# Two gate projections moved into the spectral part of a mixer, three filter spectra kept in DRAM, spectral sums in buffers of their own, Fourier and inverse tiles in alternation

## The chip, the core and the metric

The kernel runs on one core of a Trainium2 chip. Its engines work side by side, each on its own queue of instructions in a fixed order: TensorE (PE) multiplies matrices into PSUM, VectorE (DVE) and GpSimd (POOL) do elementwise work (POOL only on SBUF), ScalarE (ACT) does activations and copies, and SyncE (SP) issues the DMAs. The metric is the time of one execution on the device in microseconds, the median of several runs.

## The reference, cut to what matters

The program is a two-layer block on a sequence `x` of 512 tokens and a context of 256 tokens, 1024 features. Layer 0 mixes with a Fourier half and a hyena half, layer 1 with attention; each layer ends with a convolutional feed-forward. Only the mixer of layer 0 is changed; it is applied to `x` and to the context with the same weights:

```python
def _long_conv(u, spectrum, bias):
    L = u.shape[1]
    u32 = _f32(u)
    y = jnp.fft.irfft(jnp.fft.rfft(u32, n=2 * L, axis=1) * spectrum[None], n=2 * L, axis=1)[:, :L]
    return (y + u32 * _f32(bias)).astype(u.dtype)

def _fourier_hyena_mixer(h, w_in, w_out, conv_w, conv_b, w1, b1, w2, b2, w3, b3, w4, freq, hy_bias):
    B, L, _ = h.shape
    proj = h @ w_in
    u_f = _f32(proj[..., :D_FOURIER]).reshape(B, L, N_FOURIER_GROUPS, FOURIER_GROUP_DIM)
    y_f = jnp.fft.fft2(u_f, axes=(1, 3), norm='ortho').real.reshape(B, L, D_FOURIER).astype(h.dtype)
    u_h = _dwconv3(proj[..., D_FOURIER:], conv_w, conv_b)
    x0, x1, v = jnp.split(u_h, 3, axis=-1)
    spectrum = _hyena_filter_spectrum(L, w1, b1, w2, b2, w3, b3, w4, freq)
    y_h = x0 * _long_conv(v * x1, spectrum, hy_bias)
    return jnp.concatenate([y_f, y_h], axis=-1) @ w_out
```

`_hyena_filter_spectrum` runs a small network over the positions, weighs its two-sided output with a decay, normalizes it and takes its Fourier transform. All of this is computed with matrices of cosines and sines. `x0`, the first third of the hyena projection, is the gate: it is needed only at the very end, where it multiplies the result of the long convolution.

## The kernel before, in words

Features lie on the 128 partitions and tokens on the free axis; a tile of width `TW` = 772 holds the 512 tokens of `x`, two zeros, the 256 of the context and two zeros. Every product in full precision is three matmuls (`mm3`, L123 to L125): each operand is split into a high part (ACT, `hi`, L98) and a low part (`lo`, L103, on DVE unless POOL is named). `wload` loads a weight tile of 512 KB into one of three raw buffers (`wr`) and splits it into one of three pairs `wh` and `wl`. PSUM has three tiles `mm` of two banks and two tiles `ms` of one.

The mixer (L459) runs in this order.

- Norms, modulation and the first three input projections, in an order written out by hand (`manual_schedule`). After it the order on each engine is made by a planner, which takes work by the order of the program text where it is ready and has buffers by its own estimate of times; so later work can run ahead as filler.
- The filter: `time_tile` (L575) makes six tiles over time (4 and 5 for the context, 0 to 3 for `x`), each with a decay tile from DRAM (`dec`). Each output tile of the input projection is 48 matmuls over eight feature tiles and two column parts (`proj`, L563); `hconv` (L571) adds the three-tap convolution (`conv3`: one ACT and two DVE instructions, L322 to L324) and some modulation sums (`gemv_dve`: a 512 KB load, then per condition a DVE sum L210 and an addition L211). `filter_spec` (L432) transforms the filter, one frequency tile (`ft`) at a time, and `filter_scale` (L443) scales it into a pair `hr`, `hi`: two pairs for the context (`Hc`), four for `x` (`H`). Gate tiles 4 and 5 are projected between the time tiles, 6 and 7 after the first and second spectrum of `x` (L607).
- Eight more projections in pairs 12 + i and 8 + i (L637 to L644). `fold` multiplies the pair (POOL) and folds it (DVE, L623 and L624), and `turn` transposes it (L630) into `uTh` and `uTl`. Then `tm`, the pool of these tiles, and `hp`, the projections' input `hh` and `hl`, are closed, and the outputs `yh` and `yl` (pool `yp`) take the place of `hp`; `zero_pads` writes their pads with 32 POOL memsets.
- `spectral` (L656) transforms the folded input by one frequency tile and multiplies it by the filter: per tile two parts `c`, each with two DVE products from PSUM (L676, L677 or L680, L681, and a single row L683 for the Nyquist term `ny`), a POOL sum (L678 or L684), a high part on ACT and a low part, on DVE for `c` = 0 and on POOL for `c` = 1. It is run for the context (two tiles, `Yc`), then `inverse` (L693) and `hy_out` (L706: `e` and `s`, the gate and the split into `yh`, `yl`) four times for the context, then `spectral` for the four tiles of `x`.
- `fourier(g)` (L739) for three groups, the four inverse tiles of `x` with `hy_out`, and the fourth group. A group splits its input into `fuh` and `ful`, transforms over features into PSUM, splits that into `pqh` and `pql` (six parts: four of `x`, two of the context), transforms over time and writes its output rows. `fuh`, `ful`, `pqh` and `pql` have one buffer each.
- `res_proj` then projects with `w_out` over the eight tiles of `yh` and `yl`.

All of this shares one pool of small tiles, `S2`, with 19 buffers of 128x512 (tag `s2`): decay tiles, time tiles, `hr` and `hi`, `ny`, the `a` and `b` of the spectral products, their high and low parts (`Yc`, 8 buffers; `Y`, 16), `e` and `s`, and `e` and `y` of the Fourier groups.

Of the kernel before, what the change touches and what calls it, by code (L numbers as in the profile page):

```python
# [9 lines left out]
F32 = mybir.dt.float32  # L10
# [8 lines left out]
P = 128  # L19
D = 1024  # L20
KD = 8
# [29 lines left out]
class Builder:  # L51
# [407 lines left out]
    def mixer(self):  # L459
# [124 lines left out]
        with self.tc.issue_after(last.ins), self.tc.issue_after(last_act.ins):  # L584
# [24 lines left out]
        self.dbg("H", H, Hc, ny, nyc)  # L609
# [27 lines left out]
        for i in range(4):  # L637
# [6 lines left out]
            folded.append(fold(i, cv, cx))  # L644
        turn(3, folded.pop())
        self.dbg("u", uTh, uTl, Uf, x0)
        self.close("tm")
        self.close("hp")


        yp = self.pool("yp", side="right")
        yh = [self.t(yp, [P, TW], F32R, f"yh{m}") for m in range(KD)]
        yl = [self.t(yp, [P, TW], F32R, f"yl{m}") for m in range(KD)]
        self.zero_pads(yh + yl)

        def spectral(fts, Hs, ny, kp, km, nt):  # L656

            Y = []
            for ft, (hr, hi) in zip(fts, Hs):
# [46 lines left out]
        def hy_out(i, ps, n, c0):  # L706

            e = self.t(self.S2, [P, 512], F32, "s2")
            nc.scalar.copy(e[:, :n], ps[:, :n])
            s = self.t(self.S2, [P, 512], F32, "s2")  # L710
# [7 lines left out]
        Yc = spectral((0, 1), Hc, nyc, 4, 5, 1)  # L718
# [5 lines left out]
        Y = spectral((0, 1, 2, 3), H, ny, 0, 2, 2)  # L724
# [14 lines left out]
        def fourier(g):  # L739
# [4 lines left out]
            pqh = self.t(pF, [P, 6, 256], F32R, "pqh", 1)  # L744
            pql = self.t(pF, [P, 6, 256], F32R, "pql", 1)
            for tt0, nt, sc in ((0, 4, None), (4, 2, math.sqrt(2.0))):
                ps = self.mm()
                for a in range(nt):
                    c = 128 * (tt0 + a) + (2 if tt0 else 0)
                    self.mm3(ps[:, 256 * a : 256 * a + 256], uh[:, c : c + 128], ul[:, c : c + 128], csh, csl, True, True)  # L750
                dh = pqh[:, tt0 : tt0 + nt, :].rearrange("p a b -> p (a b)")
# [688 lines left out]
```

## Time and profile before

| | us |
|---|---|
| median of 3 runs | 1829.6 (1828.78 to 1830.51) |
| the profiled execution | 1830.64 |
| its span, first to last instruction | 1828.8 |
| PE busy in the span | 1706.3 |
| DVE busy in the span | 1022.0 |
| ACT busy in the span | 613.9 |
| POOL busy in the span | 121.3 |

The span is cut into 40 slices of 45.7 us; a digit is the busy share of a slice in tenths, 9 for 90% or more, and PEclk is the granted PE clock in the same way. A table of stretches gives each engine's busy time between two times, with the number of instructions in brackets, then the clock, the share of the DMA engines and GB/s. A row of waits names who waited, `<-` for whom, and the total in us, the number of waits and the longest. A row of the timeline is the start in us, the duration in us, engine, line, instruction, output `<-` inputs by tile name, shapes, and in brackets the idle time before it and what ended it. Times are from the span's start.

### The profile page before, as it was taken

The page shows a single profiled execution, that of the slowest core. Times are in us where ns is not written, and L with a number is a line of the kernel's source. Part 1 is how long each engine was busy: PE and PEld are TensorE (multiplying, and loading weights), DVE is VectorE, ACT ScalarE, POOL GpSimd, SP SyncE. Part 2 cuts the span into 40 slices and gives each one's busy share as a digit, 9 for nine tenths or more (in the row PEclk, how much of TensorE's full clock was granted, in tenths as well). Part 3 has the DMA queues.
Part 4 walks back from the last instruction along what each step waited for, and adds up shares of the span by engine and source line. Part 5 has one row for each costly group of instructions (what it writes and reads, how often), then busy time and mean ns, then how long its engine had stood idle before and what let it go on. Part 6 is the DMA issues. An engine that isn't in the chain of part 4 may idle for free.

```text
span 1828.8 us, 21719 instructions
## 1 busy us (share of the span) xinstructions
PE 1706.3 (93%) x8742; PEld 1326.3 (73%) x8742; DVE 1022.0 (56%) x1662; ACT 613.9 (34%) x830; POOL 121.3 (7%) x202
## 2 busy tenths in 40 slices
PE   6889975799899999999999887899998999999999
PEld 2657864787688888888888556555554777888887
DVE  3486966864898435543434554665764554444443
ACT  3332222323323212222122434655663443223231
POOL 0052113310000000000000000110110000000000
PEclk7799987899999999999999998899999999999999
DMA  9032520352355234431312310000002323322322
GB/s 351 24 127 71 171 78 30 103 173 81 116 174 176 88 104 140 147 128 70 121 47 85 117 60 24 1 12 12 12 12 70 116 72 101 104 93 92 104 75 98
DMA packets 53249, 172.83 MB, mean 95 GB/s; under 512 B 6043, under 2 KB 8925, under 8 KB 52125
## 3 DMA queue, kind: packets, MB, share of 16 engines
q1 hardware_dynamic: 53149, 171.45, 27.4%
q8 instruction: 69, 1.13, 0.2%
q14 instruction: 31, 0.25, 0.0%
HBM read 167.23 MB, written 4.19 MB: 94 GB/s over the span
## 4 chain that ended last, share of the span: by engine, by line
PE 77%; DVE 11%; ACT 5%; POOL 3%; issue 3%; DMA 1%; POOLq 0%; SPq 0%; ACTq 0%; DVEq 0%
PE mm L123 21%; PE mm L124 20%; PE mm L125 20%; PE pv L1176 2%; PE ms L234 2%; PE z L1164 2%; DVE junk L210 2%; DVE wl L103 1%; DVE S L1154 1%; PE s L1130 1%; ACT S L1145 1%; PE s L123 1%; PE s L124 1%; PE s L125 1%; POOL s L388 1%
## 5 line engine op out<-in xcount | busy, mean ns | idle before, releaser
L123 PE MATMUL mm<-hh,wh 128*128 128x512 f32 (+2 forms) x1344 | 474.7, 356 | 7.0 <-ACT wh L98 3.4
L124 PE MATMUL mm<-hl,wh 128*128 128x512 f32 (+2 forms) x1344 | 473.9, 353 | 4.9 <-DVE hl L271 4.6
L125 PE MATMUL mm<-hh,wl 128*128 128x512 f32 (+2 forms) x1344 | 473.2, 353 | 1.3 <-DVE wl L103 1.3
L98 ACT ACTIVATE wh<-wr 128x1024 fp32r<-128x1024 f32 (+2 forms) x200 | 206.2, 1031 | 717.5 <-PE mm L124 646.5
L103 DVE TENSOR_TENSOR wl<-wr,wh 128x1024 fp32r<-128x1024 f32 (+2 forms) x200 | 243.6, 1219 | 287.3 <-ACT wh L98 279.6
L123 PEld LDWEIGHTS mm<-hh,wh 128*128 128x128 f32 x1344 | 254.4, 190 | 57.1 <-issue 12.0
L124 PEld LDWEIGHTS mm<-hl,wh 128*128 128x128 f32 x1344 | 255.0, 190 | 42.9 <-DVE hl L271 7.5
L125 PEld LDWEIGHTS mm<-hh,wl 128*128 128x128 f32 x1344 | 254.5, 190 | 38.4 <-issue 2.5
L123 PE MATMUL mm<-ah,wh 128*128 128x512 f32 (+1 forms) x528 | 187.8, 356 | 0.0
L124 PE MATMUL mm<-al,wh 128*128 128x512 f32 (+1 forms) x528 | 187.7, 356 | 0.0
L125 PE MATMUL mm<-ah,wl 128*128 128x512 f32 (+1 forms) x528 | 187.3, 355 | 0.0
L210 DVE SCALAR_TENSOR_TENSOR junk<-wr,sb 128x1024 bf16<-128x1024 f32 x128 | 159.3, 1244 | 36.7 <-DMA wr<-wmodT 36.6
L808 DVE SCALAR_TENSOR_TENSOR xr<-mm,mod,xr 128x512 f32<-128x512 f32 (+1 forms) x100 | 62.2, 642 | 204.3 <-PE mm L125 204.0
L123 PEld LDWEIGHTS mm<-ah,wh 128*128 128x128 f32 x528 | 99.1, 188 | 19.2 <-DVE xr L808 2.5
L124 PEld LDWEIGHTS mm<-al,wh 128*128 128x128 f32 x528 | 99.2, 188 | 15.3 <-issue 0.8
L125 PEld LDWEIGHTS mm<-ah,wl 128*128 128x128 f32 x528 | 99.2, 188 | 14.6
L1145 ACT ACTIVATE S<-s,rks 128x512 f32<-128x512 f32 x96 | 63.4, 688 | 44.3 <-PE s L125 43.4
L1154 DVE TENSOR_TENSOR S<-S,mb 128x1536 f32<-128x1536 f32 x32 | 54.8, 1752 | 20.7 <-POOL mb L1151 20.7
L845 ACT ACTIVATE fg<-fg 128x772 f32<-128x772 f32 (+1 forms) x44 | 32.6, 741 | 100.3 <-DVE fg L324 89.3
L1176 PE MATMUL pv<-S,V 128*64 128x512 f32 x192 | 58.9, 620 | 0.0
L1164 PE MATMUL z<-S,ones 128*32 128x512 f32 x192 | 42.7, 699 | 13.7 <-ACT S L1155 11.3
L1155 ACT ACTIVATE S<-S 128x1536 f32<-128x1536 f32 x32 | 47.1, 1481 | 18.0 <-DVE S L1154 18.0
(318 smaller groups left out, 2282.6 us busy)
## 6 DMA issues: line engine op xcount, KB each, us to landing
wr<-w_up SPq DMA_DIRECT2D x88, 512.0 KB, 3.3
wr<-wmodT SPq DMA_DIRECT2D x80, 512.0 KB, 3.3
wr<-w_dn SPq DMA_DIRECT2D x32, 512.0 KB, 3.2
wm<-wmod0a SPq DMA_DIRECT2D x8, 1024.0 KB, 9.6
wr<-w_in SPq DMA_DIRECT2D x16, 512.0 KB, 3.2
wr<-w_dn SPq DMA_DIRECT2D x20, 384.0 KB, 3.1
wr<-w_out SPq DMA_DIRECT2D x12, 512.0 KB, 3.2
wr<-w_o SPq DMA_DIRECT2D x12, 512.0 KB, 3.2
```

Of the source, the lines that this page charges most:

```text
L98: self.nc.scalar.activation(dst, src, AF.Copy)
L103: (eng or self.nc.vector).tensor_tensor(dst, src, hi.bitcast(F32), op=ALU.subtract)
L123: mmul(out, wh, xh, start=start, stop=False)
L124: mmul(out, wh, xl, start=False, stop=False)
L125: mmul(out, wl, xh, start=False, stop=stop)
L210: nc.vector.scalar_tensor_tensor(junk, raw, 1.0, self.sb[:, j, :], op0=ALU.mult, op1=ALU.mult, accum_out=acc)
L808: nc.vector.scalar_tensor_tensor(x[m][:, a2:b2], ps[:, a2:b2], mod[:, 8 * sec + m, j : j + 1], x[m][:, a2:b2], op0=ALU.mult, op1=ALU.add)
L1145: nc.scalar.activation(S[j // 3][:, j % 3, :], ps, AF.Copy, scale=rs[:, 2 * j + a : 2 * j + a + 1])
L1154: v.tensor_tensor(s, s, mb3.to_broadcast([P, 3, T]), op=ALU.subtract)
L1155: nc.scalar.activation(s, s, AF.Exp)
L1164: nc.tensor.matmul(z[32 * g : 32 * g + 32, :], self.ones32, Ss[g // 2][(2 * k + g % 2) // 3][:, (2 * k + g % 2) % 3, :], start=k == 0, sto ...
L1176: nc.tensor.matmul(pv[64 * a : 64 * a + 64, :], V[:, k, 64 * h : 64 * h + 64], Ss[a][k // 3][:, k % 3, :], start=k == 0, stop=k == 5, tile ...
```

## The change

- The four decay tiles of `x` are loaded after the context's time tiles, not each at its own use.
- The scaled filter spectra of `x` for the frequency tiles 1, 2 and 3 are stored to a DRAM pool `dr` (`Hd`, six tiles) and loaded again after the context's `spectral`. All pairs stand in one dictionary `Hs` (0 and 1 for the context, 2 to 5 for `x`), and `spectral` takes a pair out as it uses it.
- Gate projections 6 and 7 leave the filter stage. 6 stands ahead of the last `turn`, 7 behind the context's `spectral`; `hp` is closed, and `yp` opened, only after 7.
- The `a` and `b` of the spectral products and the context's `e` and `s` come from a new pool `Sx` with seven buffers.
- `pqh` and `pql` become two tiles each, one for the four parts of `x` and one for the two of the context.
- The Fourier groups 1, 2 and 3 each follow an inverse tile of `x`, in place of groups 0, 1, 2, then all inverse tiles, then group 3.
- The attention's DRAM pool is renamed.

The matmuls and their operands are the same.

```diff
         def time_tile(tt):
-            if tt not in dec:
-                dec[tt] = tp()
-                nc.sync.dma_start(dec[tt], I["decay"][tt])
             pm, f = self.filter_pm(self.filter_mm(h3, tt), dec[tt], tt in (0, 4))
...
             self.load_sb()
+            for tt in range(4):
+                dec[tt] = tp()
+                nc.sync.dma_start(dec[tt], I["decay"][tt])
...
-        Hc = [self.filter_scale(self.filter_spec(ac, tb), Sc) for tb in tbc]
+
+        dr = self.pool("dr", space=bass.MemoryType.DRAM)
+        Hd = {i: [self.t(dr, [P, 512], F32, f"Hd{i}{c}") for c in range(2)] for i in range(3, 6)}
+        Hs = {i: self.filter_scale(self.filter_spec(ac, tb), Sc) for i, tb in enumerate(tbc)}
...
-        H = []
         for ft in range(4):
-            H.append(self.filter_scale(self.filter_spec(ax, self.wload(I["ftab"][ft])), S))
+            parts = self.filter_scale(self.filter_spec(ax, self.wload(I["ftab"][ft])), S)
             if ft == 0:
+                Hs[2] = parts
                 ny = self.filter_nyquist(ax, S)
-            if ft < 2:
-                hconv(6 + ft, x0[2 + ft], 1)
+            else:
+                for c in range(2):
+                    nc.sync.dma_start(Hd[2 + ft][c], parts[c])
...
             folded.append(fold(i, cv, cx))
+        hconv(6, x0[2], 1)
         turn(3, folded.pop())
         self.close("tm")
-        self.close("hp")
-
-        yp = self.pool("yp", side="right")
-        yh = [self.t(yp, [P, TW], F32R, f"yh{m}") for m in range(KD)]
-        yl = [self.t(yp, [P, TW], F32R, f"yl{m}") for m in range(KD)]
-        self.zero_pads(yh + yl)
-
-        def spectral(fts, Hs, ny, kp, km, nt):
+        Sx = self.pool("Sx", bufs=7)
+        tx = lambda: self.t(Sx, [P, 512], F32, "sx")
+
+        def spectral(fts, h0, ny, kp, km, nt):
             Y = []
-            for ft, (hr, hi) in zip(fts, Hs):
+            for ft in fts:
+                hr, hi = Hs.pop(h0 + ft)
...
                 for c in range(2):
-                    a = self.t(self.S2, [P, 512], F32, "s2")
-                    b = self.t(self.S2, [P, 512], F32, "s2")
+                    a, b = tx(), tx()
...
         def hy_out(i, ps, n, c0):
-            e = self.t(self.S2, [P, 512], F32, "s2")
+            e, s = (tx(), tx()) if n == 128 else (tp(), tp())
             nc.scalar.copy(e[:, :n], ps[:, :n])
-            s = self.t(self.S2, [P, 512], F32, "s2")
...
-        Yc = spectral((0, 1), Hc, nyc, 4, 5, 1)
+        Yc = spectral((0, 1), 0, nyc, 4, 5, 1)
+        hconv(7, x0[3], 1)
+        for i in range(3, 6):
+            Hs[i] = [tp() for _ in range(2)]
+            for c in range(2):
+                nc.sync.dma_start(Hs[i][c], Hd[i][c])
+        self.close("hp")
+        yp = self.pool("yp", side="right")
+        yh = [self.t(yp, [P, TW], F32R, f"yh{m}") for m in range(KD)]
+        yl = [self.t(yp, [P, TW], F32R, f"yl{m}") for m in range(KD)]
+        self.zero_pads(yh + yl)
         th = [self.wload(I["itab"][0])]
...
-        Y = spectral((0, 1, 2, 3), H, ny, 0, 2, 2)
+        Y = spectral((0, 1, 2, 3), 2, ny, 0, 2, 2)
+        self.close("Sx")
         self.close("pU")
...
-            pqh = self.t(pF, [P, 6, 256], F32R, "pqh", 1)
-            pql = self.t(pF, [P, 6, 256], F32R, "pql", 1)
+            pq = {}
             for tt0, nt, sc in ((0, 4, None), (4, 2, math.sqrt(2.0))):
                 ps = self.mm()
+                pq[tt0] = pqh, pql = [self.t(pF, [P, nt, 256], F32R, f"pq{q}{tt0}", 1) for q in range(2)]
...
-        for g in range(3):
-            fourier(g)
+        fourier(0)
         th = [self.wload(I["itab"][a]) for a in range(2)]
         for i in range(4):
             ps = self.ms()
             inverse((0, 1, 2, 3), Y, i, 256, th, ps)
             hy_out(i, ps, 256, 0)
-        fourier(3)
+            if i:
+                fourier(i)
```

More of the change, by code (lines that the diff above doesn't have):

```diff
@@ L750, in fourier @@
                     self.mm3(ps[:, 256 * a : 256 * a + 256], uh[:, c : c + 128], ul[:, c : c + 128], csh, csl, True, True)
-                dh = pqh[:, tt0 : tt0 + nt, :].rearrange("p a b -> p (a b)")
-                dl = pql[:, tt0 : tt0 + nt, :].rearrange("p a b -> p (a b)")
+                dh, dl = [t_.rearrange("p a b -> p (a b)") for t_ in (pqh, pql)]
                 src = ps[:, : 256 * nt]
@@ L954, in attention @@
         tok = [128 * k for k in range(4)] + [C0, C0 + 128]
-        dr = self.pool("dr", space=bass.MemoryType.DRAM)
+        dr = self.pool("dx", space=bass.MemoryType.DRAM)
         xd = self.t(dr, [KD, P, T], F32, "xd")
@@ L1240, in build @@
             nc.sync.dma_start(self.out[d], x[d][:, 0:T])
-        for n in ("xres", "h2p", "nt", "op", "dr", "psA", "sm", "W", "P0"):
+        for n in ("xres", "h2p", "nt", "op", "dx", "dr", "psA", "sm", "W", "P0"):
             self.close(n)
```

8 lines of the change are left out of this document (4 added, 4 removed).

## The prediction

> **What bounds the kernel now.** I read the page first: the engine totals, then the forty slices.
>
> ```profile
> PE 1706.3 (93%) x8742; PEld 1326.3 (73%) x8742; DVE 1022.0 (56%) x1662; ACT 613.9 (34%) x830; POOL 121.3 (7%) x202
> ...
> PE   6889975799899999999999887899998999999999
> ...
> PEclk7799987899999999999999998899999999999999
> ```
>
> TensorE (PE) is busy nearly everywhere. It is lowest in the sixth to eighth digit, 7, 5 and 7 (229 to 366 us, 45.7 us a slice), and the granted clock falls with it. That is the second half of the mixer, where all of the change lies; the 8, 8, 7, 8 later on are the attention, which isn't touched. So I cut it by stages, in the busy times of stretches:
>
> ```profile
> core 0: us, PE busy (x) PEld busy (x) DVE busy (x) ACT busy (x) POOL busy (x), PEclk, DMA share, GB/s
> 156.00:190.00 34.00, 34.00 (x171) 28.56 (x170) 22.55 (x32) 6.31 (x7) 3.69 (x3) 1.00 0.31 106
> 190.00:262.00 72.00, 69.99 (x402) 61.11 (x400) 59.15 (x102) 16.94 (x19) 10.56 (x39) 1.00 0.40 135
> 262.00:381.00 119.00, 77.44 (x448) 67.62 (x448) 87.85 (x153) 39.26 (x70) 39.27 (x46) 0.81 0.22 74
> ```
>
> The rows are the spectra of the long filter with gate projections 6 and 7 between them; the eight other hyena projections; and the spectral, Fourier and inverse part. The first is full. In the last PE stands idle for 41.6 of 119 us at clock 0.81, and no engine is full: VectorE (DVE) has 74%, GpSimd (POOL) 33%. It is a chain of waits. Who ends PE's waits there:
>
> ```profile
> PE mm L123 <- DVE s L683: 7.7, 2, 7.0
> PE mm L123 <- DVE s L681: 6.8, 2, 4.2
> PE mm L630 <- DVE tm L623: 6.7, 1, 6.7
> PE mm L125 <- DVE ful L103: 3.6, 1, 3.6
> PE mm L123 <- ACT fuh L98: 3.0, 1, 3.0
> PE mm L123 <- ACT pqh L98: 2.4, 2, 1.3
> PE mm L123 <- DVE pql L103: 2.4, 1, 2.4
> PE mm L125 <- DVE pql L103: 2.3, 1, 2.3
> ```
>
> L681 and L683 free the PSUM of a spectral product, L623 is the last fold ahead of the transpose, the others belong to the Fourier part. DVE's timeline shows why L681 and L683 are late:
>
> ```profile
> 281.16 0.67 DVE L677 TENSOR_TENSOR s<-mm,s 128x512 f32<-128x512 f32 x1
> 285.94 0.69 DVE L103 TENSOR_TENSOR s<-s,s 128x512 fp32r<-128x512 f32 x1 [4.11 <-ACT s L98]
> ...
> 287.15 0.68 DVE L681 TENSOR_TENSOR s<-mm,s 128x512 f32<-128x512 f32 x1
> 292.77 0.29 DVE L711 TENSOR_TENSOR s<-s,ms 128x128 f32<-128x128 f32 x1 [4.94 <-ACT s L709]
> ...
> 298.86 0.69 DVE L676 TENSOR_TENSOR s<-mm,s 128x512 f32<-128x512 f32 x1
> ```
>
> DVE ends the context's products at 287.8 and starts the first of x at 298.9, after the context outputs, although the matmuls of that tile ended by 280.0. The code says what is missing: of the 19 buffers of `s2` the filter spectra of x hold 8, `ny` 1 and the context's result 8, and two are left.
>
> **What the change does, step by step.** The profiled execution took 1830.6 us (span 1828.8 and 1.8 around it), 1.0 above the median of 1829.6; the sum is made against it and then lowered by that 1.0.
>
> *Taken out upstream.* Projection 6 runs from 156.02 to 164.47 and projection 7 from 170.07 to 178.53 in PE's timeline, each between filter spectra and without a hole: 8.45 + 8.46 = 16.9 us fall out. The four spectra then stand back to back, 5.8 us of matmuls each; beside each DVE has one weight split (1.2 to 2.0) and two scalings (0.7 each), ScalarE (ACT) one split of 1.1, POOL one sum of 1.3. If the cover were gone, one spectrum would wait 1.1 + 1.2 = 2.3 us for its split. I take 0. **-16.9** (-16.9 to -14.6).
>
> *Projection 6 put ahead of the last transpose.* Its 8.45 us meet the wait of 6.74 us for the fold: **+1.7** (0 to +8.45; the fold's own wait is the nearest row).
>
> *Projection 7 put behind the context's products.* PE's own waits from 277 to 288 are 0.7, 0.7 and 4.2 us, and DVE and POOL set the pace there, so I charge no PE time for it. What it and projection 6 bring to the other engines is charged: per projection a split (L103, 1.22), two convolution steps (L323 and L324, 1.01 and 1.02), and one modulation sum in two halves of 1.24, 0.08 and 0.18 (L210, its accumulator read, L211), so 6.3 us of DVE, 12.5 for both; ACT's 2 x 2.0 disappear in its 80 idle us. DVE has 31 idle of 119. Ends 0 (all in DVE's holes) and +12.5 (all on the chain); by the nearest row, a DVE 74% busy whose work is the chain's at about every other step, half: **+6.3**.
>
> A rule of the Trainium skill speaks against this step: SBUF — State Buffer, section "Who interferes with whom", says that a VectorE instruction with two SBUF inputs and a GpSimd one that reads SBUF lock each other out for a whole instruction. The trace agrees in kind: in the stretch the weight split has a mean of 1601 ns against 1219 over the kernel, and POOL's L678 takes 1503 against 1.29 us where it is undisturbed. By those rows the six added instructions with two SBUF inputs lose 6 x 0.38 = 2.3 us, inside the half above; by the rule each could wait for a whole sum of 1.3 us, 7.7 in all, and the forecast would stand 5.4 us higher.
>
> *The pads behind projection 7.* `hp` now closes after it, so the 32 memsets of `zero_pads(yh + yl)` wait for its matmuls, on POOL, whose queue also carries the spectral sums. Before, they ran while POOL had nothing else (255 to 262). Ends 0 and a whole projection, +8.45; the planner sees both, so I take **+2.0**.
>
> *Three filter spectra through DRAM.* Six stores and six loads of 256 KB. The nearest rows, on SP, are the copies of x to and from DRAM, 2.0 and 5.1 us to landing; issuing takes SP 0.4 each. A store waits for its scaling (DVE 0.7 and POOL 1.3 after the matmuls); behind it on SP stand weight loads, needed 8.4 us later and landing in 3.2. A load is needed only after the first tile of x, and the queues move 20 GB/s in 262 to 288. I take 0 (0 to +5.1).
>
> *What the freed buffers give.* With `a` and `b` and the context's `e` and `s` in seven tiles of their own and six spectra away, the products of x can follow those of the context at 287.8: 11.0 us earlier. The context outputs need DVE for 4 x 1.42 = 5.7 us in that time anyway, so **-5.3** (-11.0 to 0: after the reloads 17 of 19 `s2` buffers are held again, and the second tile of x needs the context's result to be gone).
>
> *Spectral sums not held by the next low part.* Within x's four tiles (298.9 to 339.7, 10.2 us each) DVE waits 1.8 and 4.2 us for ACT before a low part, with the next products queued behind it; that wait and the 4.1 in the context are the 10.1 us that DVE's waits show for L103 after ACT. With seven tiles the next products go first. POOL has 3 x 1.3 = 3.9 us a tile, so the 4.1, where POOL itself was late, stays: **-6.0** (-10.1 to 0).
>
> *Fourier and inverse alternate, `pqh` and `pql` in two parts.* The waits for `fuh`, `ful`, `pqh` and `pql` in the list above sum to 13.7 us. An inverse tile is 24 matmuls at 0.12 = 2.9 us, enough for most of one such wait, but the planner mixed the two already (PE runs inverse matmuls at 324, 329, 349 and 364). The two parts let the next group's copies start before the second inverse is read. **-5.0** (-13.7 to 0).
>
> *Decay tiles loaded earlier.* The time tiles are paced by POOL's four operations per tile; 0 (-3.8, the one hole of PE there, to +3.8). *Modulation sums as filler.* Six ran in DVE's idle places from 335 to 382 (12 x 1.26 us); what no longer fits slides into 381 to 420, where DVE is busy 17.7 of 39: 0 (0 to +4, three of L210).
>
> Sum: -16.9 + 1.7 + 6.3 + 2.0 - 5.3 - 6.0 - 5.0 = -23.2, so 1807.4 on the profiled execution and **1806** as a median. A cross-check: the last stretch becomes 119 + 16.9 - 23.2 = 112.7 us. DVE's work in it without the filler (15.2 + 0.9 + 4.8) is 67.0, with the two projections 79.5: 71%, close to the 74% that it holds now.
>
> **The rivals.** *DVE takes the place of the waits.* The projections' DVE work lies on the chain in full and the freed buffers give only the earlier start: -16.9 + 1.7 + 12.5 - 5.3 = -8.0, so 1822. For it speaks DVE at 34 of 41 us in 299 to 340; against it that its slow splits there (2.3, 3.4 for two) overlap POOL.
>
> *The holes close.* All buffer waits and Fourier waits go and the projections are free: -16.9 + 1.7 - 11.0 - 10.1 - 13.7 = -50, so 1780; DVE would then be 93% busy for 86 us, which no stretch here shows. The matmuls would speed up as well: at 0.23 and 0.12 us a start the 448 need some 58 us, not 77. TensorE: Matmul & The Clock Gate, in "Why this matters for your kernels", asks for no idle gap over about 3 us; the 0.81 beside gaps of 7.0, 6.7 and 4.2 agrees, and by that rule this rival would also give the clock back.
>
> *Projection 7 stands in the chain* (slower). `hp` can't become `yp` before its last matmul, the context outputs write `yp`, and the reloads hold 17 of 19 buffers until those outputs free the context's result. If the planner puts the projection ahead of products that are ready, its 8.45 us and all DVE work are serial and the buffer gains are void: -16.9 + 1.7 + 12.5 + 8.45 = +5.8, so 1835. It decides when the time from the end of the last paired projection to the unbroken `w_out` passes 119 + 16.9 = 136 us.
>
> *It does nothing*: what leaves upstream comes back whole, 1830.
>
> **Numbers.** The forecast (1792 to 1816) gets 0.55; holes closing (1780 to 1792) 0.10; DVE as the bound (1816 to 1826) 0.17; nothing 0.04; projection 7 in the chain 0.14. Faster is 0.82, same 0.04, slower 0.14, where 0.2% (3.7 us) is about what can be told from no change. The range 1786 to 1828 leaves out half of the closing holes (0.05), the slower case (0.14) and the top of "nothing" (0.01).
>
> **What would show it.** The four filter spectra back to back without a wait, and the first of the eight other projections some 16.9 us earlier; no 6.7 us wait before L630; DVE's L676 of x's first tile within 2 us of the context's last product or of a POOL sum; L680 ahead of the low part; the stretch to `w_out` at 105 to 118 us with a clock above 0.9. Wrong would be: PE waiting for POOL's memsets or for a reload, DVE over 85% busy there, or a stretch past 136 us.

## The result and the profile after

The changed kernel takes 1810.9 us (median of six runs, 1808.2 to 1817.4) beside 1829.2 us for the kernel before (1827.6 to 1831.6): ratio 0.9906, 95% interval 0.9884 to 0.9928, or 18.3 us less. The forecast was 1806, with a range of 1786 to 1828, so both the sign and the range held. The sum behind it held in its first half only, as the experiments show.

The profiled execution of the changed kernel took 1817.4 us (span 1815.6). It is the longest of the six, so differences in the trace come out smaller than the median's: 13.2 us less than the profiled execution before. The forty slices, on the page after, once more with PE and its granted clock:

```profile
PE 1707.5 (94%) x8742; PEld 1331.4 (73%) x8742; DVE 1019.9 (56%) x1662; ACT 614.2 (34%) x830; POOL 118.2 (7%) x202
...
PE   6889996899999999999999887899998999999999
...
PEclk7799997999999999999999998899999999999999
```

The trough that was 7, 5, 7 is now 9, 6, 8. The stretches answer to the three of before: the spectra, the eight projections (with projection 6 at their end), and the spectral, Fourier and inverse part (with projection 7 in it). Columns: length, then each engine's busy time and instructions, the granted clock, DMA share and GB/s.

```profile
145.00:170.00 25.00, 25.00 (x106) 18.85 (x105) 23.84 (x31) 4.48 (x5) 3.88 (x3) 1.00 0.43 150
170.00:253.00 83.00, 80.33 (x451) 70.18 (x450) 69.23 (x121) 18.83 (x20) 11.04 (x9) 0.98 0.45 152
253.00:361.00 108.00, 80.45 (x477) 72.84 (x477) 86.05 (x150) 40.79 (x69) 33.36 (x66) 0.83 0.28 93
```

The spectra stand back to back without a hole. The last stretch is 108 us long where it was 119, although it now holds 8.6 us more of projection. But its clock is still 0.83, and PE still stands idle for 27.55 us. The list of who ends PE's waits there has changed (engine and line waited for; us in total, times, longest):

```profile
PE mm L123 <- ACT fuh L98: 14.2, 1, 14.2
PE mm L123 <- ACT pq L98: 4.9, 4, 2.8
PE mm L125 <- DVE pq L103: 2.8, 4, 0.9
PE mm L123 <- ACT uTh L98: 2.0, 1, 2.0
```

The waits of 7.0, 6.7 and 4.2 us are gone. In their place stands a single hole of 14.2 us, between the last spectral product of x (293.9) and the first Fourier product (308.1). VectorE's timeline after shows where x's products went. The columns are start, duration, engine, line, operation, and in brackets the idle time before and what ended it:

```profile
265.79 0.67 DVE L680 TENSOR_TENSOR sx<-mm,s 128x512 f32<-128x512 f32 x1
...
283.17 0.43 DVE L103 TENSOR_TENSOR yl<-sx,yh 128x256 fp32r<-128x256 f32 x1 [0.48 <-ACT yh L98]
285.76 0.69 DVE L675 TENSOR_TENSOR sx<-mm,s 128x512 f32<-128x512 f32 x1 [2.17 <-PE mm L125]
286.37 0.68 DVE L676 TENSOR_TENSOR sx<-mm,s 128x512 f32<-128x512 f32 x1
286.97 0.68 DVE L679 TENSOR_TENSOR sx<-mm,s 128x512 f32<-128x512 f32 x1
287.57 0.68 DVE L680 TENSOR_TENSOR sx<-mm,s 128x512 f32<-128x512 f32 x1
289.19 0.69 DVE L103 TENSOR_TENSOR s<-sx,s 128x512 fp32r<-128x512 f32 x1 [0.95 <-ACT s L98]
```

The four products of a tile now go ahead of the low part (L680 before L103), as forecast. But x's first product again comes after all four context outputs, 19.3 us behind the context's last product where it was 11.0. What DVE waits for last is now PE (2.17 us), which has projection 7 (261.6 to 270.2) and the context's inverses (270.0 to 281.4) ahead of x's matmuls in its order.

From there GpSimd has the most to do, three passes of 1.27 us and a wait of 0.74 for a tile of 4.45 us, and ScalarE's queue passes the end of the sums on to the Fourier part. GpSimd's timeline for x's last tile, then ScalarE's:

```profile
302.80 1.27 POOL L677 TENSOR_TENSOR sx<-sx,sx 128x512 f32<-128x512 f32 x1
304.02 1.26 POOL L683 TENSOR_TENSOR sx<-sx,sx 128x512 f32<-128x512 f32 x1
306.02 1.27 POOL L103 TENSOR_TENSOR s<-sx,s 128x512 fp32r<-128x512 f32 x1 [0.74 <-ACT s L98]
```

```profile
305.31 0.63 ACT L98 ACTIVATE s<-sx 128x512 fp32r<-128x512 f32 x1 [0.59 <-POOL sx L683]
305.85 0.40 ACT L98 ACTIVATE csh<-wr 128x256 fp32r<-128x256 f32 x1
306.16 1.15 ACT L98 ACTIVATE cth<-wr 128x520 fp32r<-128x520 f32 x2
307.21 0.83 ACT L98 ACTIVATE fuh<-x 128x772 fp32r<-128x772 f32 x1
```

x's sums take 21.5 us (285.8 to 307.3) where they took 40.8. But the copies that open the Fourier part stand behind the last of them in ScalarE's queue; before, the Fourier products ran among the sums.

**A way to compare traces.** The change begins to act at the decay loads and the spectra, but executions already differ ahead of that: PE reaches its 251st matmul, in the first projections, between 75.7 and 81.3 us. So each trace is cut at three matmuls: A, the 251st; B, the first spectral product of the context (line 123 on `uTh`); C, the 201st of the output projection. In us, all from the profiled executions, with x's first product on VectorE, the end of GpSimd's last pass over its sums and the first Fourier product counted from B. The rest runs from C to the last matmul. The last two columns are PE's idle time and its granted clock between B and C:

```
kernel                      A to B  B to C   rest   x's first   sums end   Fourier  PE     PE
                                                    product                starts   idle   clock
before                      189.6   142.0   1412.1    28.0        68.8       41.9   34.2   0.87
changed kernel              174.6   141.0   1414.8    29.8        51.4       52.2   25.6   0.87
projections alone           171.7   140.9   1414.0    31.7        66.7       45.5   21.5   0.85
projections back            195.9   138.6   1411.9    26.9        48.8       49.6   29.6   0.84
sums in the shared ring     172.4   142.9   1413.8    31.7        67.0       45.7   23.2   0.86
no alternation              171.6   136.9   1414.0    29.3        50.9       51.7   23.3   0.88
projection 6 alone          183.8   147.7   1411.4    30.7        71.5       44.6   29.2   0.80
projection 7 alone          181.9   138.9   1412.6    30.1        65.4       44.1   20.9   0.86
x first                     174.1   140.8   1411.9    13.0        51.0       51.8   23.5   0.85
x first, no alternation     173.5   136.1   1413.2    13.1        50.9       51.7   24.6   0.90
shared ring, no alternation 174.6   141.0   1413.8    31.6        66.7       45.4   21.1   0.85
low part on VectorE         174.4   137.9   1414.2    29.8        50.9       53.7   25.9   0.89
joined halves               173.0   136.8   1412.5    30.0        51.6       52.4   25.2   0.90
tables early                173.1   141.8   1414.6    29.6        58.9       42.1   26.2   0.87
```

Two of these traces differ by some 3 us in A to B where nothing between A and B differs (171.6 to 174.6), so a single number here is good to about that.

Where the sums have tiles of their own, the Fourier part starts 0.8 us behind GpSimd's last pass (2.8 with the low part on VectorE), unless its tables are made early; in the shared ring it starts 21 to 27 us ahead of it. ScalarE's queue shows where the copies stand, not why. The planner may rank them last, or they may have had to wait for the space of `Sx` and `pU`, which are closed just ahead of them; no run separates the two.

### The profile page after: what moved, and what is told of

Read it like the earlier page. It is cut to its first block, busy times and chain, and to the rows that moved or that the text cites. A ratio compares the mean times of both kernels' runs of the same rounds, so it can differ in the third digit from the quotient of the medians.

```text
span 1815.6 us, 21750 instructions
## 1 busy us (share of the span) xinstructions
PE 1707.5 (94%) x8742; PEld 1331.4 (73%) x8742; DVE 1019.9 (56%) x1662; ACT 614.2 (34%) x830; POOL 118.2 (7%) x202
## 4 chain that ended last, share of the span: by engine, by line
PE 78%; DVE 11%; ACT 4%; issue 3%; POOL 2%; DMA 1%; POOLq 0%; SPq 0%; ACTq 0%; DVEq 0%
PE mm L123 22%; PE mm L125 21%; PE mm L124 21%; PE pv L1186 2%; DVE junk L210 2%; PE ms L234 2%; PE z L1174 2%; DVE wl L103 1%; PE s L1140 1%; DVE S L1164 1%; ACT S L1155 1%; PE s L123 1%; PE s L124 1%; PE s L125 1%; DMA wr<-wmodT 1%
## 5 line engine op out<-in xcount | busy, mean ns | idle before, releaser
L103 DVE TENSOR_TENSOR wl<-wr,wh 128x1024 fp32r<-128x1024 f32 (+2 forms) x200 | 242.7, 1214 | 282.2 <-ACT wh L98 274.3
```

Source lines behind the costliest of these rows:

```text
L103: (eng or self.nc.vector).tensor_tensor(dst, src, hi.bitcast(F32), op=ALU.subtract)
```

## The experiments

Each kernel was timed in turn with the kernel before on the same chip. The ratios are to those runs.

**The projections alone.** The kernel before, with projections 6 and 7 moved and the halves' pool closed later; decay tiles at their own use, no DRAM, no tiles of their own, no alternation, joined halves.

```
-            if ft < 2:
-                hconv(6 + ft, x0[2 + ft], 1)
...
+        hconv(6, x0[2], 1)
         turn(3, folded.pop())
...
-        self.close("hp")
...
         Yc = spectral((0, 1), Hc, nyc, 4, 5, 1)
+        hconv(7, x0[3], 1)
+        self.close("hp")
```

> The kernel before with one part of the change alone: projections 6 and 7 at their new places, and hp closed behind 7. Theory A (projection 7 stands in the spectral chain, so that only projection 6 is nearly free): 16.9 us leave upstream, 1.7 come back at the last transpose and 8.5 in front of the context outputs, so 6 to 7 us faster than before, about 1822 to 1823. Theory B (both fall into holes; the whole gain of the change is theirs): 15 to 18 us faster, about 1811 to 1814, like the changed kernel. Theory C (their VectorE work lies on the chain in full and the 19 buffers stay short): within 4 us of before, 1825 to 1833. In the trace A has the context outputs starting after projection 7, and VectorE's first product of x after them.

Measured: 1812.8 us (1808.0 to 1812.9), ratio 0.9915 (0.9902 to 0.9927), 15.6 us less. Most of the change's gain is here, with none of its other parts. Who ends PE's waits in this kernel:

```profile
PE mm L123 <- DVE s L673: 4.5, 2, 4.1
PE mm L125 <- DVE ful L103: 4.1, 1, 4.1
```

The 6.7 us wait ahead of the last transpose is gone, and so is one of the two long waits for PSUM, that of 7.0 us. The other (4.2 before) and the one for `ful` (3.6 before) stay.

**The projections back.** The changed kernel with both projections between the spectra again, all other parts kept.

```
+            if ft < 2:
+                hconv(6 + ft, x0[2 + ft], 1)
...
-        hconv(6, x0[2], 1)
         turn(3, folded.pop())
...
-        hconv(7, x0[3], 1)
```

> The changed kernel with projections 6 and 7 back between the filter spectra; all else stays. Theory A: 16.9 us come back upstream and the hole of 6.7 us before the last transpose returns, while 2 x 8.5 us of projections leave the spectral part: 6 to 7 us slower than the changed kernel, about 1817. Theory B: the whole gain is lost, about 1826 to 1830. Theory C: 0 to 3 us slower, 1811 to 1814. The first product of x starts 8 us sooner after the context's products in A.

Measured: 1829.2 us (1825.3 to 1833.8), ratio 1.0011 (1.0001 to 1.0021). The other parts together bring nothing: in the table B to C is 3.4 us shorter than before, A to B 6.3 longer. PE's waits:

```profile
PE mm L123 <- ACT fuh L98: 14.6, 1, 14.6
PE mm L635 <- DVE tm L628: 6.7, 1, 6.7
```

The wait for the fold is back (L635 is this kernel's line for the transpose), and the hole ahead of the Fourier part is there as well. So that hole comes from the other parts and not from projection 7. Theory B, "the projections carry the whole gain", stands; a projection 7 that stands serial in the chain does not.

**The sums in the shared ring.** The changed kernel with `a`, `b`, `e` and `s` in `s2`.

```
-                    a, b = tx(), tx()
+                    a, b = tp(), tp()
...
-            e, s = (tx(), tx()) if n == 128 else (tp(), tp())
+            e, s = tp(), tp()
```

> The changed kernel with the products a and b and the context's e and s back in the s2 buffers (the filter spectra still go through DRAM). Theory A (the seven buffers halve the time of a spectral tile of x, from 10.2 to 5.4 us, but the Fourier part no longer runs beside it and PE stands 14.2 us): tiles of x at 8 to 10 us each again, the hole of 14.2 us shorter than 8, time 3 to 8 us above the changed kernel, 1814 to 1819. Theory D (the recorded sum: the buffers bring 5.3 + 6.0): 11 us above, 1822. Theory E (DRAM alone frees enough buffers): within 3 us of the changed kernel.

Measured: 1812.2 us (1806.8 to 1813.3), ratio 0.9909 (0.9894 to 0.9924), the changed kernel's time. By the table, the sums end 15.6 us later after B (67.0 against 51.4), the Fourier part starts 6.5 us earlier (45.7 against 52.2), and B to C comes out at 142.9 against 141.0. Theory E has the time, but not the way to it: a tile of x takes 8 to 9 us again, as theory A had it, so DRAM alone doesn't free the sums. The 3 to 8 us that A set on it don't show.

**No alternation.** The changed kernel with Fourier tiles 0, 1, 2 ahead of the inverses and 3 behind them.

```
-        fourier(0)
+        for g in range(3):
+            fourier(g)
...
-            if i:
-                fourier(i)
+        fourier(3)
```

> The changed kernel with Fourier groups 0, 1, 2, then the four inverse tiles, then group 3, as before; pqh and pql stay in two parts. Theory A and D (the alternation is worth most of the 5.0 us): 3 to 5 us above the changed kernel, 1814 to 1816, with PE waits of over 8 us for the Fourier copies. Theory F (the planner mixes both orders anyway): within 2 us, 1809 to 1813.

Measured: 1805.2 us (1804.9 to 1810.9), ratio 0.9888 (0.9874 to 0.9903): 5.6 us under the changed kernel by the medians, 3.3 by the ratios, whose intervals overlap, and 4.1 us in B to C. PE's waits in this kernel:

```profile
PE mm L123 <- ACT fuh L98: 14.2, 1, 14.2
PE mm L125 <- DVE pq L103: 2.6, 4, 0.9
...
PE mm L123 <- ACT pq L98: 1.5, 3, 0.9
```

The hole of 14.2 us is the same. What alternation adds are the waits for the split of the first product on ScalarE, 4.9 us in the changed kernel against 1.5. From B to C alternation adds 2.3 us of idle time and 1.8 us of busy time to PE. None of the theories had this: A and D expected a slower kernel, F one within 2 us.

**One projection at a time.** The first edit above, with projection 6 alone and then with projection 7 alone.

```
-            if ft < 2:
+            if ft == 1:
                 hconv(6 + ft, x0[2 + ft], 1)
...
+        hconv(6, x0[2], 1)
         turn(3, folded.pop())
```

> The kernel before with projection 6 alone moved to the last turn; projection 7 stays between the spectra, and nothing else is changed. Theory 'each projection pays its own length': 8.4 us out of the stretch of the spectra, 1.7 us back at the last turn since a projection of 8.4 us fills a wait of 6.74: -6.7, and up to -8.4 if the splits' waits shrink too: ratio to before 0.9954 to 0.9963. Rival 'projection 6 carries it all, since it has a hole to go to and projection 7 has none': -13 to -16, ratio 0.991 to 0.993.

```
-            if ft < 2:
+            if ft < 1:
                 hconv(6 + ft, x0[2 + ft], 1)
...
         Yc = spectral((0, 1), Hc, nyc, 4, 5, 1)
+        hconv(7, x0[3], 1)
+        self.close("hp")
```

> The kernel before with projection 7 alone moved behind the context's spectral products (the halves' pool closed behind it); projection 6 stays between the spectra. Theory 'each projection pays its own length': 8.4 us out of the spectra, and in the new place it fills PE time that stood idle anyway (41.9 us of idle in that stretch before): -7 to -9, ratio 0.995 to 0.996. Rival 'projection 7 stands in the chain there': its 8.6 us come back whole, ratio 0.999 to 1.001.

Measured: projection 6 alone 1824.4 us (1822.0 to 1826.4), ratio 0.9968 (0.9956 to 0.998), 5.3 us less. Projection 7 alone 1818.3 us (1814.7 to 1819.4), ratio 0.993 (0.9917 to 0.9942), 11.4 us less. The two add up to 16.7, the two together gave 15.6. Both rivals fall: projection 7 doesn't stand in the chain, and projection 6 doesn't carry it all. That each pays just its own length isn't right either, since projection 7 brings more than its 8.5 us. In B to C, which it makes 8.6 us of matmuls longer, the trace has 138.9 us against 142.0: the wait of 7.0 us for PSUM shrinks to 0.4, and PE's idle time falls from 34.2 to 20.9. With projection 6 alone, that stretch is 147.7, in the longest of its six runs. PE is idle for 5.0 us less there than before, but at a granted clock of 0.80 against 0.87 the same matmuls keep it busy for 118.5 us, where they took 107.7.

**x first.** x's spectral tiles 0 and 1 ahead of projection 7; first in the changed kernel, then also without alternation.

```
         Yc = spectral((0, 1), 0, nyc, 4, 5, 1)
+        load_H(3)
+        Y = spectral((0, 1), 2, ny, 0, 2, 2)
         hconv(7, x0[3], 1)
+        load_H(4)
...
-        Y = spectral((0, 1, 2, 3), 2, ny, 0, 2, 2)
+        load_H(5)
+        Y += spectral((2, 3), 2, ny, 0, 2, 2)
```

> The changed kernel with x's spectral tiles 0 and 1 (products and sums) put ahead of projection 7, tiles 2 and 3 where they were; the two late spectra come back from DRAM one tile later each. Theory G, 'the faster sums end into the 14.2 us hole': ScalarE's queue has the tables' copies and the first Fourier tile's copy behind the last sum's high part, so the Fourier part starts when POOL is done. Two of four tiles of 4.4 us POOL time start some 20 us earlier, so the last sum ends 6 to 9 us earlier, the hole shrinks from 14.2 to 5 to 8 us and the time falls 6 to 9 us below that of the changed kernel: ratio to before 0.986 to 0.988. Rival H, 'the hole is cover for something else': projection 7's convolution and the context's outputs are now late behind the sums in ScalarE's and VectorE's queues, and the time comes out within 2.5 us of the changed kernel or above it: ratio 0.989 to 0.993.

> The same as the run before, and the Fourier tiles 0, 1, 2 ahead of the inverses and 3 behind them, as in the kernel before the change. Theory G: 6 to 9 us below the run with that order alone (1805.2 beside 1828.4, ratio 0.9888), ratio 0.984 to 0.9855. Rival H: within 2.5 us of it, 0.9875 to 0.990. If the order of the Fourier tiles matters by itself, this run lies below the one before by 3 us or more; if not, within 2.5 us.

Measured: 1809.0 us (1807.5 to 1813.3), ratio 0.9887 (0.9869 to 0.9904); without alternation 1805.0 us (1804.0 to 1806.9), ratio 0.9863 (0.9849 to 0.9876). PE's waits in the first of them:

```profile
PE mm L123 <- ACT fuh L98: 8.5, 1, 8.5
...
PE ms L124 <- DVE wl L103: 3.0, 1, 3.0
PE ms L123 <- DVE sx L710: 2.8, 1, 2.8
```

The hole shrank by 5.7 us, to just above the 5 to 8 us of theory G. But what G made of it is wrong: x's first product comes 16.8 us earlier after B (13.0 against 29.8), and yet the last sum ends where it did (51.0 against 51.4), since tiles 2 and 3 of x still follow the context's outputs (VectorE starts tile 2 at 40.6 after B). The context's inverses now wait, for the split of their table and for the outputs, behind x's products and projection 7's convolution on VectorE, and the idle time has moved from the hole to them. B to C is 140.8 against 141.0, and 136.1 against 136.9 without alternation. The two ratios lie between the ranges of G and H; by B to C, and with medians 1.9 and 0.3 us below those of the kernels without this edit, rival H is the nearer.

**The square closed.** The shared ring, and no alternation (both edits above).

> The changed kernel with the spectral sums' tiles back in the shared ring and the Fourier tiles 0, 1, 2 ahead of the inverses: projections, DRAM and split tables stay. With the kernels already timed it closes a square: own tiles and alternation (the changed kernel, 0.9906), shared ring and alternation (0.9909), own tiles and no alternation (0.9888). Theory J, 'own tiles pay only where the Fourier tiles stand together; alternation eats that gain': ratio 0.991 to 0.9925, like the projections alone (0.9915), so that own tiles are worth 4 to 7 us without alternation and nothing with it. Rival K, 'own tiles are worth nothing in either order, alternation alone costs 5 us': ratio 0.988 to 0.990.

Measured: 1810.5 us (1807.7 to 1816.9), ratio 0.9899 (0.9883 to 0.9915). That lies below theory J's range and at the upper edge of rival K's, and its interval reaches into both: the times don't decide it. By B to C the four corners are 141.0 (own tiles, alternation), 142.9 (shared ring, alternation), 136.9 (own tiles, none) and 141.0 (shared ring, none). Read so, own tiles give 4.1 us without alternation and 1.9 with it, and alternation costs 4.1 and 1.9. That is close to what the traces can tell. Nor is it idle time that own tiles save. The stretch from B to C, first with own tiles and no alternation, then with the shared ring and none:

```profile
248.49:385.34 136.85, 113.60 (x669) 101.10 (x669) 99.78 (x179) 45.00 (x76) 37.64 (x106) 0.88 0.35 117
255.34:396.30 140.96, 119.88 (x669) 106.68 (x670) 102.44 (x179) 45.02 (x76) 41.42 (x106) 0.85 0.36 114
```

With one long hole PE is idle for 23.3 us, with many short waits for 21.1. But the same matmuls keep it busy for 113.6 us at a granted clock of 0.88, and for 119.9 at 0.85.

**The low part on VectorE.** The kernel without alternation, with the low part of x's second sum moved off GpSimd.

```
-                    self.lo(ylo, a, yhi, nc.gpsimd if c else None)
+                    self.lo(ylo, a, yhi, nc.gpsimd if c and nt == 1 else None)
```

> The changed kernel without alternation (0.9888), and the low part of x's second sum on VectorE instead of GpSimd: GpSimd does two passes of 1.27 us a tile instead of three with a wait of 0.74 between, VectorE four passes of 0.67 to 1.08 us more. Theory L, 'the hole of 14.2 us ends when GpSimd has done the sums': 2.0 us a tile come out of its pace of 4.4, VectorE's pace of 3.7 to 4.5 a tile takes over, the last sum ends 2 to 6 us earlier, the hole is 8 to 12 us and the time 2 to 6 us lower, ratio 0.9855 to 0.988. Rival M, 'the pace is set by ScalarE's and VectorE's hand-over as much': the hole stays at 13 to 15 us and the time within 1.5 us, ratio 0.988 to 0.9895.

Measured: 1811.7 us (1810.8 to 1813.1), ratio 0.9900 (0.9887 to 0.9912), 6.5 us above the same kernel without it by the medians, 2.2 by the ratios and 1.0 in B to C: no gain by any of them. Theory L falls; rival M is the nearer, though hole and time lie somewhat above its ranges. GpSimd's timeline:

```profile
293.99 1.27 POOL L677 TENSOR_TENSOR sx<-sx,sx 128x512 f32<-128x512 f32 x1
297.75 1.27 POOL L683 TENSOR_TENSOR sx<-sx,sx 128x512 f32<-128x512 f32 x1 [2.49 <-DVE sx L680]
298.98 1.27 POOL L677 TENSOR_TENSOR sx<-sx,sx 128x512 f32<-128x512 f32 x1
```

GpSimd has two passes a tile and now waits 2.49 us for VectorE; a tile takes 5.0 us, not 4.45. VectorE holds L680 behind two low parts, the first of which waits 0.9 us for ScalarE. GpSimd's last pass ends where it did (50.9 after B), but it is now the sum itself, which ended at 48.8 without this edit; the hole grows to 15.8 us. So GpSimd wasn't the only one at its limit.

**Joined halves.** The kernel without alternation, with `pqh` and `pql` as one pair for both parts.

```
-            pq = {}
+            pqh = self.t(pF, [P, 6, 256], F32R, "pqh", 1)
+            pql = self.t(pF, [P, 6, 256], F32R, "pql", 1)
```

> The changed kernel without alternation (0.9888), and the first product's halves back in one pair of tiles for x and the context. Theory N, 'the split tables carry what this order has over the projections alone (4.9 us)': ratio 0.9905 to 0.992, the waits ahead of the first product's use come back. Rival O, 'the split tables are worth nothing': within 1.5 us, ratio 0.988 to 0.9895, and what the order has over the projections alone comes from the sums' own tiles.

Measured: 1806.0 us (1804.2 to 1809.2), ratio 0.9873 (0.9858 to 0.9888); B to C is 136.8 against 136.9. Rival O stands: the split is worth nothing.

**Tables early.** The kernel without alternation, with `csh`, `csl`, the high half of the cosine table and the first Fourier tile's halves made ahead of x's sums. They need 12.4 KB of each partition, so the sums' own ring shrinks to four tiles and `b` goes to the shared one.

```
-        Sx = self.pool("Sx", bufs=7)
+        Sx = self.pool("Sx", bufs=4)
...
-                    a, b = tx(), tx()
+                    a, b = tx(), tp()
...
+        table(I["cs128"], csh[:], csl[:], 256)
+        self.hi(fu0[0], Uf[0])
+        self.lo(fu0[1], Uf[0], fu0[0])
         Y = spectral((0, 1, 2, 3), 2, ny, 0, 2, 2)
```

> The changed kernel without alternation (0.9888), and the tables of the Fourier part that its first products need (the 128-point table's two halves, the cosine table's high half) and the first Fourier tile's halves made ahead of x's spectral sums, in memory of their own; to make room, the sums' ring has 4 tiles and the second product of each sum lies in the shared ring. Theory P, 'the hole before the Fourier part ends where it does because ScalarE's queue has those copies behind the last sum': the first tile's 18 products (3.9 us) run right behind the spectral products, the hole of 14.2 us splits, the first product's halves are split some 4 to 5 us earlier, and the time falls 3 to 5 us, ratio 0.986 to 0.987. Rival Q, 'the sums' own pace still sets when ScalarE and VectorE come to the split of the first product, and the smaller ring slows them': within 1.5 us or slower, ratio 0.988 to 0.991.

Measured: 1811.4 us (1807.8 to 1812.9), ratio 0.9888 (0.9869 to 0.9908). Rival Q stands. PE's waits:

```profile
PE mm L123 <- ACT pq L98: 10.0, 3, 8.7
PE mm L123 <- DVE s L680: 7.9, 2, 4.3
```

The Fourier products do start 42.1 us after B instead of 51.7. But PE then waits 8.7 us for the split of their result, which ScalarE makes behind the last sum, and with four tiles the sums fall back into the old order: L680 waits behind a low part again, a tile takes 6.6 us, and the last sum ends at 58.9 instead of 50.9. The two effects weren't separated; what early tables would give beside a ring of seven wasn't tried, for lack of memory.

The best version run is "x first, no alternation": 0.9863 (0.9849 to 0.9876), under the changed kernel's 0.9906 (0.9884 to 0.9928) with no overlap. What it has over that kernel is mostly the alternation undone: against the run with that edit alone (0.9888, 0.9874 to 0.9903) its interval overlaps.

## Why the prediction was right, and where its sum was not

*Taken out upstream and projection 6 in the fold's wait* (-16.9 and +1.7): right. A to B fell from 189.6 to 174.6, by 15.0 where the two terms say 15.2. That they agree so well is partly luck. The stretch of the spectra gave 16.2, the way to them 3.3 more that the sum didn't have (the projections alone give these too), and the other projections, with 6 among them, cost 4.5 (1.8 in the projections alone) where 1.7 was forecast. The spectra take 145.6 to 170.4 without a hole, so no split came uncovered, and the wait of 6.74 us is gone.

*Projection 7 behind the context's products* (+6.3 for half of the DVE work): mis-sized, and the largest miss on that side. That PE would not pay for it was right. But the DVE work costs nothing either: B to C fell by 3.1 us with projection 7 moved alone and by 1.1 with both. PE's idle time there went from 34.2 us to 20.9 and 21.5. I charged the engine that was 74% busy by its share of the chain; its instructions fell into waits that were there anyway. The Trainium skill's rule in SBUF — State Buffer, "Who interferes with whom", is borne out here too: the split of x's first table starts at 269.08 beside a GpSimd sum and takes 2.31 us where the mean is 1.21. It isn't what sets the end: it is done at 271.4, and x's matmuls start at 281.2, behind the inverses.

*The pads behind projection 7* (+2.0): the 32 memsets end at 273.5, about 1.0 us in all, and GpSimd then stands idle for 13.7 us. 0, the low end.

*The freed buffers, x's products earlier* (-5.3): wrong. The chain from missing buffers to a late first product was read from VectorE's timeline and the buffer count, and no run bears it out. In the changed kernel PE has projection 7 and the inverses ahead of x's matmuls. With the projections back and own tiles, x's first tile is through PE at 282.3, and still its first product comes behind three context outputs, 26.9 us after B where it was 28.0. VectorE's timeline there:

```profile
287.77 1.08 DVE L103 TENSOR_TENSOR s<-sx,s 128x512 fp32r<-128x512 f32 x1 [3.06 <-ACT s L98]
292.45 0.29 DVE L710 TENSOR_TENSOR sx<-sx,ms 128x128 f32<-128x128 f32 x1 [3.60 <-ACT sx L709]
...
299.94 0.69 DVE L676 TENSOR_TENSOR sx<-mm,s 128x512 f32<-128x512 f32 x1
```

So the place in VectorE's queue holds it, with idle time ahead of it. Whether the planner chose that place, or had to because x's first `a` and `b` come behind the context's eight `e` and `s` in the same ring of seven, isn't separated. "x first" changes the order, and the time hardly falls: 13.0 instead of 29.8 us to x's first product, and the same end of the sums.

*Sums not held by the low part* (-6.0): the mechanism was right and far larger than its bound. x's four tiles take 21.5 us instead of 40.8. What was wrong is that this would reach the end of the stretch. The Fourier part starts 52.2 us after B where it started at 41.9, since its first copies now stand behind the sums in ScalarE's queue. Of 19.3 us in the sums, 4.1 are left in B to C without alternation and 1.9 with it, and without alternation they are left as a higher granted clock and not as less idle time.

*Alternation and halves in two parts* (-5.0): wrong in sign for the first and nothing for the second. Taking alternation out gave 4.1 us in B to C, 3.3 by the ratios and 5.6 by the medians; joining the halves again gave 0.1. The changed kernel's four waits for `pq` on ScalarE show the place; why the order that was written out leaves them open and the planner's own order fills them was only argued ("the planner mixed the two already" was in the prediction, and the term was taken all the same).

*DRAM, decay tiles, modulation sums* (0 each): mostly borne out, none measured by itself. From A to x's first spectrum it is 64.2 us in the projections alone, which loads the decay tiles late, and 63.8 to 64.3 in the changed kernel and those with its early loads and moved projections. No PE wait ends with a reload; the stores land after a median of 3.3 us and the loads after 3.1. One number speaks against 0: with the projections back, A to B takes 195.9 us against 189.6 before, with the same matmuls. About half of it is busy time at a lower granted clock (0.94 against 0.97), half idle time. With one trace each, whether the stores and early loads cost that stays open.

So the terms behind B were to give -8.0 and gave -1.0 in the trace. (Behind C, where nothing was changed, the changed kernel's trace is 2.7 us longer; the medians differ by 5 us more than the traces.) In the place of +8.3 for the projections (+6.3, +2.0) stands -1.1, the run that moves them alone; in the place of -16.3 for all the rest stands +0.1, what the changed kernel has beyond it. The forecast hit within 5 us because what the projections free upstream was sized right, and, by luck, because these two errors ran against each other.

*Of the signs to look for*: the back-to-back spectra, the earlier first projection (19.5 us, of which 3.3 had been won ahead of the spectra), the missing wait ahead of the transpose, L680 ahead of the low part, and the stretch at 108 us came as written. L676 within 2 us of the context's last product and a clock above 0.9 (it is 0.83) did not. Of the rivals, "holes close" fell to the new hole, "projection 7 stands in the chain" to its own run, and "DVE takes the place of the waits" to the runs that moved projection 7, whose added DVE work left B to C no longer. "It does nothing" fell to the time itself.

What stays open is what limits B to C as a whole. In fourteen kernels it lies between 136.1 and 147.7 us, though the sums end anywhere from 48.8 to 71.5 us after B and the Fourier part starts from 41.9 to 53.7. No single one of these times goes with it: the tables early start the Fourier part 10 us sooner than the kernel without alternation and end 4.9 us later.

The table's last columns tell part of it, and the sum had no term for it: the granted clock. In the eleven kernels with projection 7 behind B, the same matmuls keep PE busy for 111.5 us (clock 0.90) to 119.9 (0.85), while its idle time lies between 20.9 and 26.2. The shortest stretches have the least busy time, and not the least idle time. Each trace is one execution, so how steady these clocks are, and which holes cost how much clock, isn't shown.

## What to carry to other kernels

Work taken from a full stretch into one with idle time on every engine is the safe part of a change: it gave 15.6 of the 18.3 us, and its instructions on the other engines cost nothing that B to C shows. Making one link of a chain faster is worth only what the next stage can start earlier, so look at what stands behind that link in the other engines' queues: here 19 us off the sums became a 14 us hole. Read the granted clock beside the idle time: of two kernels here with the same matmuls, the one with 2.2 us more idle time is 4.1 us shorter. Try the parts of a compound change alone, since here one part cost about what another gave.

## What the runs showed of the hardware

The start of the program varies with the clock, ahead of any change. The first 76 us of the changed kernel, and then of "x first, no alternation", in which the same instructions stand (columns as above):

```profile
0.00:76.00 76.00, 53.58 (x220) 28.77 (x221) 35.07 (x89) 26.41 (x49) 1.20 (x36) 0.71 0.60 225
```

```profile
0.00:76.00 76.00, 53.58 (x252) 30.34 (x253) 36.76 (x92) 28.32 (x50) 1.20 (x36) 0.82 0.61 225
```

PE is busy for the same 53.58 us, but it gets through 252 matmuls at a granted clock of 0.82 and through 220 at 0.71. In the first of the two, one stretch at half clock lasts from 32.0 to 69.5 us. This is up to 5.6 us at the 251st matmul, a third of what the whole change is worth.

Half clock followed a hole of 2.16 us too (214.25 to 216.41, ahead of a transpose), with no other hole since 196.3:

```profile
214.20:216.30 2.10, 0.05 (x1) 0.00 (x0) 2.10 (x4) 1.91 (x2) 1.78 (x2) 1.00 0.14 57
216.30:219.70 3.40, 3.29 (x13) 3.03 (x14) 3.37 (x10) 0.81 (x1) 0.00 (x0) 0.50 0.15 35
219.70:221.00 1.30, 1.30 (x9) 1.13 (x9) 1.30 (x2) 0.00 (x0) 0.00 (x0) 0.99 0.83 309
```

The Trainium skill, TensorE: Matmul & The Clock Gate, section "Why this matters for your kernels", asks for no idle gap over about 3 us. Here a gap of 2.16 us was enough for one spell of 3.4 us at 0.50.
